# Two of four weight sums, and two of four activation sums, put on GpSimd in the feed-forward units

## The chip, the cores and the metric

The kernel runs on one core of a Trainium2 chip. A core has TensorE (PE: matrix products, results go to PSUM), VectorE (DVE) and ScalarE (ACT) for elementwise work, GpSimd (POOL), and SyncE (SP), which here only starts transfers. Each engine works through its own list of instructions in order and waits on semaphores for the others. The metric is the device time of one execution in microseconds (us). The kernel before takes 2019.6 us (median of three runs, 2017.96 to 2023.13).

## The reference

The reference is a decoder trunk of two layers over 512 tokens of width 1024 in float32. Each layer is: half a SwiGLU feed-forward, a mixer, half a SwiGLU feed-forward. The mixer of layer 0 is an SSD head group beside an mLSTM head group, that of layer 1 a sparse attention with a top-k selection. The change touches the four feed-forwards alone:

```
def swiglu(h, w_gate, w_up, w_down):
    return (jax.nn.silu(h @ w_gate) * (h @ w_up)) @ w_down

x = x + 0.5 * swiglu(rms_norm(x, ffn_norm[l, i]), w_gate[l, i], w_up[l, i], w_down[l, i])
```

The inner width is 2816, so `w_gate` and `w_up` are 1024 x 2816 and `w_down` is 2816 x 1024.

## The kernel before, in words

**Numbers in two parts.** Every operand of a product is split into a high part (rounded to the format that PE takes) and a low part (the rest), and `mm3` (lines 280 to 282) makes three matmuls of one product: high x high, high x low, low x high. A block of weights lands in a `raw` buffer (a ring of 4, `NRAW`), and its two parts go to a `form` buffer (a ring of 5, `NFORM`). There are two ways to make a form. `parts` lets ACT write the high part (line 500) and DVE the low part as the difference (line 502). The other, marked `summed`, lets ACT write the negated high part into the low place (line 529), then a transfer from POOL's queue adds the raw block to it (line 530), and ACT writes the high part (line 531).

**Units.** A feed-forward has 11 units of 256 inner columns, in groups of 4, 4 and 3 (`GROUPS`). Units 0 and 1 multiply plainly (`unit`). Units 2 to 10 (`unit_seven`), and the down projection of each group in two halves (`down`), use a 2 x 2 scheme with seven products in place of eight (`seven`). This makes 9 + 6 = 15 sevens in a feed-forward and 60 in the kernel. A seven takes four raw blocks b11, b21, b12, b22 and multiplies, in turn, forms of b11 (with A11), of b12 - b11 (S1), of b22 - b11' (S2), of b21 (A12), of b22 - b12 (S3), of b22 (S4), and of b21 - t2 (A22); b11' is the first difference and t2 the second. In the first half of a down projection the A12 product comes second. The four differences of raw blocks are `less` (line 648), which writes the first into b11, the second into a box t2, the third into b12, and the fourth into t2 again. Forms of b21 and b22 are made the `summed` way, the other five by `parts`.

**Streams.** The activations that a seven of gate and up multiplies with are seven forms of the normed stream, `xf`, made once in a feed-forward by `xforms` (two calls): four sums of 128 x 512 blocks in the tiles `ft`, numbered 4 (S1), 5 (S2), 6 (S3) and 7 (S4), and splits of all seven. Those of a down projection come from the hidden block of each unit (`forms`: sums of 128 x 256 blocks in `ft`, parts in `hid`). The down projection of a group can't begin to use a unit's `hid` before the unit's own last products have been evacuated (c12 and c21 in `unit_seven`), multiplied, and split.

**What sets the order.** The feed-forwards (and the attention) are not issued as they are written. `Plan` collects steps with an engine, a price and the keys that they read and write; `order` runs a list schedule over them: at each turn the step that can start first on its engine is taken, and by the earliest due time among those; PE keeps the written order of each stream. `issue` then hands the steps to the engines in that order. The prices are `v` for DVE (0.15 us + 1.05 ns for each element of a row) and `p` for POOL (0.1 us + 2.5 ns). The plan knows no contention between engines. The helper `vtt` (line 492) adds a two-input operation to DVE, or to POOL if its last argument is true; all these operations have line 495 in the profile. POOL's queue holds the 136 adding transfers of line 530, the adds of the squares for the norm (line 495, tile `ssq`), and work of the mixers. The kernel's ring of raw blocks has just the four of one seven, so each block of the next seven is loaded when its predecessor in the ring was last read.

Of the kernel before, what the change touches and what calls it, by code (L numbers as in the profile page):

```python
# [17 lines left out]
T = 512  # L18
# [195 lines left out]
class Trunk:  # L214
# [274 lines left out]
    def t(self, us, issue, reads, writes):  # L489
        self.plan.add("tensor", us, issue, reads, writes)  # L490
# [81 lines left out]
    def xforms(self, q0, tiles):  # L572


        (t, tk), (u, uk) = self.place(), self.place()
        which, xT, rrow, nc = self.which, self.xT, self.rrow, self.nc
        block = [lambda i=i: t()[:, 2 * i : 2 * i + 2] for i in range(4)] + [lambda i=i: u()[:, 2 * i : 2 * i + 2] for i in range(4)]
        bk = [[tk(2 * i), tk(2 * i + 1)] for i in range(4)] + [[uk(2 * i), uk(2 * i + 1)] for i in range(4)]
        for q in range(2):
            for m in range(2):  # L580
                k = 2 * (q0 + q) + m
                self.v(T, lambda q=q, m=m, k=k: nc.vector.scalar_tensor_tensor(
                    t()[:, 4 * m + q : 4 * m + q + 3 : 2], xT[:, k].rearrange("p (a b) -> p a b", a=2), self.gain(which, k),
                    rrow.rearrange("p (a b) -> p a b", a=2), op0=ALU.mult, op1=ALU.mult,
                ), self.xk(k) + ["rrow"], [tk(4 * m + q), tk(4 * m + q + 2)])
        key = lambda i, part, q: ("xf", self.count["xf"], i, part, q)

        def split(form, i):
            self.parts(
                T, lambda: tiles[form]()[:, 0, q0 : q0 + 2], lambda: tiles[form]()[:, 1, q0 : q0 + 2], block[i],  # L590
                [key(form, 0, q0), key(form, 0, q0 + 1)], [key(form, 1, q0), key(form, 1, q0 + 1)], bk[i],
            )

        tt = lambda o, x, y, op: self.vtt(T, block[o], block[x], block[y], op, bk[o], bk[x] + bk[y])
        split(self.A11, 0)
        tt(4, 1, 3, ALU.add)
        split(self.S1, 4)
        tt(5, 4, 0, ALU.subtract)
        split(self.S2, 5)
        split(self.A12, 2)  # L600
        tt(6, 0, 1, ALU.subtract)
        split(self.S3, 6)
        tt(7, 2, 5, ALU.subtract)
        split(self.S4, 7)
        split(self.A22, 3)
        return [
            (lambda i, q=q: (tiles[i]()[:, 0, q], tiles[i]()[:, 1, q]), lambda i, q=q: [key(i, 0, q), key(i, 1, q)])
            for q in (q0, q0 + 1)
        ]
# [11 lines left out]
    def seven(self, raws, xf, late, kept, evac):  # L621

        nc = self.nc
        b11, b21, b12, b22 = raws
        c11, c12, c21, c22 = evac
        nq = len(xf)
        i, two = "sum", self.box
        t2 = i, two[:, 0 : nq * 256].rearrange("p (n w) -> p n w", w=256)  # L630

        def mul(ps, block, form, start, summed=False, f=None, ss=(0, 1)):
            j, f = made = f or self.made(block, summed)
            ps, psk = ps
            for s in ss:
                col = slice(s * P, (s + 1) * P)
                for q in range(nq):
                    self.times(
                        ps, psk, s, (j, lambda q=q, col=col: (f[:, 0, q, col], f[:, 1, q, col])),
                        lambda q=q: xf[q][0](form), xf[q][1](form), start and q == 0, q == nq - 1, not start, H, 0.355,  # L640
                    )
            return made

        def keep(to, ps):
            (to, tok), (ps, psk) = to, ps
            self.s(T, lambda: nc.scalar.activation(to(), ps()[:, :, 0:H], AF.Copy), [(*psk, 0), (*psk, 1)], tok)

        def less(o, x, y):
            n = nq * 256
            self.vtt(n, lambda: o[1], lambda: x[1], lambda: y[1], ALU.subtract, [("raw", o[0])],  # L650
                     [("raw", x[0]), ("raw", y[0])])
            return o

        A, D = self.pair("pA", "pA"), self.pair("pD", "pB")
        mul(A, b11, self.A11, True)
        keep(kept[0], A)
        if late:
            B = self.pair("pB", "pB")
            mul(B, b21, self.A12, True, True)
            c11(B, kept[0])  # L660
            mul(D, less(b11, b12, b11), self.S1, True)
            keep(kept[2], D)
            mul(A, less(t2, b22, b11), self.S2, False)
            keep(kept[1], A)
            f22 = mul(D, b22, self.S4, False, True, ss=(0,))
            mul(A, less(b12, b22, b12), self.S3, False)
            c22(A, kept[2])
            mul(D, b22, self.S4, False, f=f22, ss=(1,))
            c12(D, kept[1])
        else:  # L670
            mul(D, less(b11, b12, b11), self.S1, True)
            keep(kept[2], D)
            mul(A, less(t2, b22, b11), self.S2, False)
            keep(kept[1], A)
            B = self.pair("pB", "pB")
            mul(B, b21, self.A12, True, True)
            c11(B, kept[0])
            mul(A, less(b12, b22, b12), self.S3, False)
            c22(A, kept[2])
            mul(D, b22, self.S4, False, True)  # L680
            c12(D, kept[1])
        mul(A, less(t2, b21, t2), self.A22, False)
        c21(A, None)

    def unit_seven(self, raws, xf):
# [1208 lines left out]
```

## Time and profile before

| what | us |
|---|---|
| median of three runs | 2019.6 |
| profiled execution, its own time | 2019.29 |
| its span, first to last instruction | 2017.6 |
| PE busy | 1984.4 (98%) |
| DVE busy | 1581.4 (78%) |
| ACT busy | 1170.2 (58%) |
| POOL busy | 270.1 (13%) |

The granted TensorE clock is 0.992 of full speed over the span. Busy time is the union of an engine's instructions; the ends of matmuls are modelled, so a busy PE can still have had small gaps. In the timeline a row gives the start, the length (of all instructions merged in it), engine, line, operation, what it writes and reads, and in brackets the idle time before it with what ended it. The feed-forwards lie at 0 to 345 us, 762 to 1092 us, 1093 to 1434 us and 1677 us to the end.

### The profile page before, as it was taken

What the parts mean: (1) busy time and instruction counts of PE and PEld (TensorE: products, weight loads), DVE (VectorE), ACT (ScalarE), POOL (GpSimd) and SP (SyncE); (2) the same over time, 40 slices, a digit from 0 to 9 for tenths busy, and PEclk for the clock granted to TensorE, in tenths of its full rate; (3) what the DMA queues carried; (4) which work ended last, traced back from release to release, by engine and by line L of the source; (5) the groups of instructions that cost most, each with busy time, mean ns of one, the idle gap of its engine ahead of it and who ended that gap; (6) DMA issues with size and microseconds to landing.
All of it is one profiled execution on the core that took longest, in us unless ns stands there. A gap on an engine that the chain in (4) does not pass through costs nothing.

```text
span 2017.6 us, 34412 instructions
## 1 busy us (share of the span) xinstructions
PE 1984.4 (98%) x13892; PEld 1800.6 (89%) x13892; DVE 1581.4 (78%) x2340; ACT 1170.2 (58%) x1716; POOL 270.1 (13%) x335
## 2 busy tenths in 40 slices
PE   8999999999999999999999999999999999999998
PEld 6999999787788888999998899999965678999998
DVE  6898878886547648988888898978679847988886
ACT  6666657442345434666565575756667644757565
POOL 1000101321101011010002010101215321101010
PEclk9999999999999999999999999999899999999999
DMA  7556566433331232666565356656754202656564
GB/s 210 136 148 167 150 164 148 125 107 115 103 96 63 82 97 63 168 157 162 155 152 149 94 148 167 161 153 160 191 116 105 53 16 69 157 158 165 150 168 115
DMA packets 214439, 265.49 MB, mean 132 GB/s; under 512 B 14140, under 2 KB 187400, under 8 KB 214280
## 3 DMA queue, kind: packets, MB, share of 16 engines
q1 hardware_dynamic: 193632, 190.87, 30.5%
q0 software_dynamic: 20448, 72.36, 19.2%
q8 instruction: 109, 1.79, 0.4%
q14 instruction: 50, 0.41, 0.1%
q10 hardware_dynamic: 200, 0.06, 0.0%
HBM read 188.77 MB, written 2.14 MB: 95 GB/s over the span
## 4 chain that ended last, share of the span: by engine, by line
PE 86%; DVE 5%; DMA 4%; issue 2%; ACT 1%; POOL 1%; SPq 0%; ACTq 0%; POOLq 0%; DVEq 0%
PE pA L281 9%; PE pA L280 9%; PE pA L282 9%; PE pD L280 5%; PE pD L281 5%; PE pD L282 5%; PE pB L280 2%; PE pB L281 2%; PE pB L282 2%; DMA form<-raw 2%; PE po L280 2%; PE po L282 2%; PE po L281 2%; PE ptok L280 2%; PE pu L282 2%
## 5 line engine op out<-in xcount | busy, mean ns | idle before, releaser
L502 DVE TENSOR_TENSOR form<-raw,form 128x1024 fp32r<-128x1024 f32 (+1 forms) x327 | 388.0, 1191 | 113.2 <-ACT form L500 112.3
L500 ACT ACTIVATE form<-raw 128x1024 fp32r<-128x1024 f32 (+1 forms) x327 | 334.6, 1027 | 177.3 <-DVE raw L495 120.6
L280 PE MATMUL pA<-xf,form 128*128 128x256 f32 x1152 | 322.1, 280 | 0.0
L281 PE MATMUL pA<-xf,form 128*128 128x256 f32 x1152 | 321.8, 279 | 0.0
L282 PE MATMUL pA<-xf,form 128*128 128x256 f32 x1152 | 321.4, 279 | 0.0
L495 DVE TENSOR_TENSOR raw<-raw 128x1024 f32<-128x1024 f32 (+2 forms) x241 | 283.6, 1180 | 17.4 <-DMA raw<-in_ffn_w_down 8.6
L530 POOL DMA_DIRECT2D form<-raw x136 | 116.9, 860 | 1202.7 <-ACT form L529 1142.4
L529 ACT ACTIVATE form<-raw 128x1024 fp32r<-128x1024 f32 (+1 forms) x136 | 140.1, 1031 | 140.3 <-PE pD L282 77.4
L280 PEld LDWEIGHTS pA<-xf,form 128*128 128x128 f32 x1152 | 216.4, 188 | 0.2
L282 PEld LDWEIGHTS pA<-xf,form 128*128 128x128 f32 x1152 | 216.1, 188 | 0.0
L281 PEld LDWEIGHTS pA<-xf,form 128*128 128x128 f32 x1152 | 215.8, 187 | 0.2
L281 PE MATMUL pA<-hid,form 128*128 128x256 f32 x704 | 198.6, 282 | 2.8 <-DVE hid L502 2.8
L280 PE MATMUL pA<-hid,form 128*128 128x256 f32 x704 | 198.8, 282 | 0.5 <-ACT hid L500 0.4
L282 PE MATMUL pA<-hid,form 128*128 128x256 f32 x704 | 197.4, 280 | 0.0
L280 PE MATMUL pD<-xf,form 128*128 128x256 f32 x576 | 161.2, 280 | 0.0
L281 PE MATMUL pD<-xf,form 128*128 128x256 f32 x576 | 161.2, 280 | 0.0
L282 PE MATMUL pD<-xf,form 128*128 128x256 f32 x576 | 161.0, 280 | 0.0
L495 DVE TENSOR_TENSOR ft<-ft 128x256 f32<-128x256 f32 (+2 forms) x288 | 146.1, 539 | 4.6 <-ACT ft L748 1.2
L531 ACT ACTIVATE form<-raw 128x1024 fp32r<-128x1024 f32 (+1 forms) x136 | 138.6, 1021 | 0.0
L281 PEld LDWEIGHTS pA<-hid,form 128*128 128x128 f32 x704 | 132.3, 188 | 4.7 <-DVE hid L502 4.6
L280 PEld LDWEIGHTS pA<-hid,form 128*128 128x128 f32 x704 | 132.6, 188 | 1.3 <-ACT hid L500 0.6
L282 PEld LDWEIGHTS pA<-hid,form 128*128 128x128 f32 x704 | 132.3, 188 | 0.0
(447 smaller groups left out, 5191.5 us busy)
## 6 DMA issues: line engine op xcount, KB each, us to landing
form<-raw POOLq DMA_DIRECT2D x120, 512.0 KB, 5.6
raw<-in_ffn_w_gate SPq DMA_DIRECT2D x88, 512.0 KB, 3.8
raw<-in_ffn_w_up SPq DMA_DIRECT2D x88, 512.0 KB, 4.0
raw<-in_ffn_w_down SPq DMA_DIRECT2D x64, 512.0 KB, 4.4
raw<-in_hy_w_in SPq DMA_DIRECT2D x44, 512.0 KB, 3.5
raw<-in_ffn_w_down SPq DMA_DIRECT2D x32, 384.0 KB, 3.4
raw<-in_hy_w_out SPq DMA_DIRECT2D x16, 512.0 KB, 3.3
form<-raw POOLq DMA_DIRECT2D x16, 384.0 KB, 4.2
```

The costliest lines, as they stand in the source:

```text
L280: mm(out, l[0], r[0], start=start, stop=False)
L281: mm(out, l[0], r[1], start=False, stop=False)
L282: mm(out, l[1], r[0], start=False, stop=stop)
L495: (self.p if pool else self.v)(n, lambda: e.tensor_tensor(out(), x(), y(), op=op), reads, writes)
L500: self.s(n, lambda: nc.scalar.activation(hi(), src(), AF.Copy), srck, hik)
L502: n, lambda: nc.vector.tensor_tensor(lo(), src(), hi().bitcast(F32), op=ALU.subtract), srck + hik, lok
L529: self.s(n, lambda: nc.scalar.activation(f()[:, 1], raw, AF.Copy, scale=-1.0), rawk, lok)
L530: self.plan.add("gpsimd", 0.85, lambda: nc.gpsimd.dma_start(f()[:, 1], raw, accum_op=ALU.add), rawk + lok, lok, 5.5)
L531: self.s(n, lambda: nc.scalar.activation(f()[:, 0], raw, AF.Copy), rawk, hik)
```

## The change

The third and the fourth of the four differences of raw blocks in every seven (b22 - b12, and b21 - t2), and the sums numbered 6 and 7 in `xforms` (for S3 and S4), are given to POOL. The plan prices them with `p` and orders all steps anew. What is computed is the same.

```
-        tt = lambda o, x, y, op: self.vtt(T, block[o], block[x], block[y], op, bk[o], bk[x] + bk[y])
+        tt = lambda o, x, y, op: self.vtt(T, block[o], block[x], block[y], op, bk[o], bk[x] + bk[y], o in (6, 7))
...
-        def less(o, x, y):
+        def less(o, x, y, pool=False):
             n = nq * 256
             self.vtt(n, lambda: o[1], lambda: x[1], lambda: y[1], ALU.subtract, [("raw", o[0])],
-                     [("raw", x[0]), ("raw", y[0])])
+                     [("raw", x[0]), ("raw", y[0])], pool)
             return o
...
-            mul(A, less(b12, b22, b12), self.S3, False)
+            mul(A, less(b12, b22, b12, True), self.S3, False)
...
-            mul(A, less(b12, b22, b12), self.S3, False)
+            mul(A, less(b12, b22, b12, True), self.S3, False)
...
-        mul(A, less(t2, b21, t2), self.A22, False)
+        mul(A, less(t2, b21, t2, True), self.A22, False)
```

In the changed program's lists POOL has 120 more operations on raw blocks (104 of 128 x 1024, 16 of 128 x 768, the last group of a feed-forward having three units) and 16 more on `ft` (128 x 512); DVE has as many fewer. On POOL they stand between the adding transfers, mostly one after each; where a group begins two stand together. The order of DVE, ACT and of SP's loads changes throughout the feed-forwards; that of PE only at the seam from the first feed-forward to the mixer of layer 0 and in the attention.

## The prediction

> **What bounds the kernel now.** I read the page's busy shares first, then the stages of the feed-forwards by windows, then the chain that ended last, and the timelines of one seven and of one group end.
>
> ```profile
> PE 1984.4 (98%) x13892; PEld 1800.6 (89%) x13892; DVE 1581.4 (78%) x2340; ACT 1170.2 (58%) x1716; POOL 270.1 (13%) x335
> ```
> ```profile
> 105.00:147.00 42.00, 40.90 (x343) 40.50 (x342) 38.83 (x49) 25.03 (x31) 3.43 (x4) 1.00 0.54 143
> ...
> 1184.00:1224.00 40.00, 39.64 (x332) 39.44 (x331) 36.78 (x46) 23.34 (x30) 3.40 (x4) 1.00 0.56 147
> 1224.00:1303.00 79.00, 79.00 (x673) 79.00 (x672) 66.48 (x82) 51.99 (x69) 6.87 (x9) 1.00 0.66 168
> ...
> sum 1270.00, PE 1264.42 PEld 1236.21 DVE 1090.10 ACT 804.78 POOL 112.13; mean PE 46.83 PEld 45.79 DVE 40.37 ACT 29.81 POOL 4.15
> ```
>
> The columns are span, then busy time of PE, weight loads, DVE, ACT and POOL. The last row sums 27 stretches that cover nearly all of the four feed-forwards: PE is idle for 5.6 of 1270 us there. From 1224 to 1303 us, four sevens, it is idle for nothing while DVE is busy for 84%. So relief of DVE can't buy much in these stages: at most those 5.6 us. Where PE does idle is where a group's down projection begins (the first two rows). The chain that ended last passes through DVE just there:
>
> ```profile
> 1400.39 0.70 DVE ft L495
> 1401.15 0.57 issue
> 1401.72 0.95 DVE form L502
> 1402.67 0.87 DVE raw L495
> 1403.54 0.61 DVE hid L502
> 1404.20 0.39 PE pA L281
> ```
>
> PE waits for the last unit's `hid`, and DVE makes it after a form and a raw difference. This is what the change touches: DVE is not the bound on average, but its latency is at twelve group ends (three in each feed-forward).
>
> **The change, part by part.** First, the work moved.
>
> ```profile
> L495 DVE TENSOR_TENSOR raw<-raw 128x1024 f32<-128x1024 f32 x208 | 253.2, 1220 | 16.4 <-DMA raw<-in_ffn_w_down 7.7 <-DMA raw<-in_ffn_w_up 6.7
> ...
> L495 DVE TENSOR_TENSOR ft<-ft 128x512 f32<-128x512 f32 x104 | 68.5, 686 | 0.9
> ...
> L495 DVE TENSOR_TENSOR raw<-raw 128x768 f32<-128x768 f32 x32 | 30.3, 953 | 1.0 <-DMA raw<-in_ffn_w_down 0.9
> ```
>
> DVE loses 104 x 1.220 + 16 x 0.953 + 16 x 0.686 = 126.9 + 15.2 + 11.0 = 153 us. On POOL no operation of 1024 elements is in the trace; the nearest are the adds of squares:
>
> ```profile
> L495 POOL TENSOR_TENSOR ssq<-ssq x23: 729/1597/2156, 350.1 to 1672.1; 128x512 f32<-128x512 f32 x17, 128x256 f32<-128x256 f32 x6
> ```
> ```profile
> L404 POOL TENSOR_TENSOR ssq<-ssq,sq x7: 1295/1345/1855, 709.0 to 759.5; 128x512 f32<-128x512 f32 x7
> ```
>
> The quickest take 0.729 us for 256 elements (the first row's minimum) and 1.295 us for 512, which is 2.21 ns for each further element; so I estimate 2.43 us for 1024 and 1.86 us for 768. POOL gains 104 x 2.43 + 16 x 1.86 + 16 x 1.295 = 303 us. It has the room (270 of 2017.6 us busy), so this by itself costs nothing.
>
> Second, what an operation of POOL does to DVE. Where the sums of squares run beside a busy DVE:
>
> ```profile
> 350.08 5.11 POOL L495 TENSOR_TENSOR ssq<-ssq 128x512 f32<-128x512 f32 x3 [5.10 <-ACT ssq L809]
> ```
> ```profile
> 349.87 0.74 DVE L798 SCALAR_TENSOR_TENSOR xgn<-raw,xgn 128x512 fp32r<-128x512 f32 x1
> 350.53 1.79 DVE L858 SCALAR_TENSOR_TENSOR raw<-ft,raw 128x512 f32<-128x512 f32 x1
> 352.24 0.68 DVE L495 TENSOR_TENSOR ft<-pA,ft 128x512 f32<-128x512 f32 x1
> 352.84 2.90 DVE L798 SCALAR_TENSOR_TENSOR xgn<-raw,xgn 128x512 fp32r<-128x512 f32 x2
> 355.66 0.68 DVE L858 SCALAR_TENSOR_TENSOR raw<-ft,raw 128x512 f32<-128x512 f32 x1
> ```
>
> The same DVE operation takes 1.79 us beside POOL and 0.68 us after it; two of line 798 take 2.90 us in place of 2 x 0.74. The one that reads PSUM and SBUF (`ft<-pA,ft`) stays at 0.68 us. So DVE operations with both inputs in SBUF wait for POOL's. DVE lost 1.11 + 1.42 = 2.53 us to three POOL operations that alone take 3 x 1.295 = 3.89 us: 0.65 us for each us of POOL. For 303 us that is 197 us lost against 153 us saved: DVE is not relieved but delayed by some 44 us, and its share of the 1270 us goes from 86% to about 89%. It still has room on average, and PE stays the bound in the middle of a group. The Trainium skill, SBUF — State Buffer, section Who interferes with whom, has the rule: a DVE instruction with two SBUF inputs contends with a GpSimd instruction that reads SBUF, and the later one blocks until the first is through. The trace agrees (1.79 against 0.68 us, and 0.68 us with one PSUM input).
>
> Third, the middle of a group, one seven of gate and up.
>
> ```profile
> 1246.99 0.28 PE L280 MATMUL pD<-xf,form 128*128 128x256 f32 x1
> ...
> 1269.60 0.28 PE L280 MATMUL pA<-xf,form 128*128 128x256 f32 x1
> ```
> ```profile
> 1260.38 1.23 DVE L495 TENSOR_TENSOR raw<-raw 128x1024 f32<-128x1024 f32 x1
> ...
> 1262.13 1.21 DVE L495 TENSOR_TENSOR raw<-raw 128x1024 f32<-128x1024 f32 x1
> 1263.36 1.23 DVE L502 TENSOR_TENSOR form<-raw,form 128x1024 fp32r<-128x1024 f32 x1
> 1264.62 1.23 DVE L495 TENSOR_TENSOR raw<-raw 128x1024 f32<-128x1024 f32 x1
> ```
> ```profile
> 1262.78 0.86 POOL L530 DMA_DIRECT2D form<-raw  x1 [12.79 <-ACT form L529]
> ```
>
> The four DVE rows are b22 - b11', b22 - b12 (moved), the low part of the S2 form, and b21 - t2 (moved). The S2 form is ready at 1264.6 us and PE starts on it at 1269.60 us: 5.0 us of slack, the least that I found on the weights' side. With the moved difference on POOL as soon as b22 has landed, b22 - b11' can wait for it (up to 2.43 us); the low part after it isn't blocked again, since b21 - t2 overwrites t2 and must wait for that low part. So at most half the slack goes. The adding transfer of b21, queued on POOL at 1262.78 us, now stands behind the moved difference (ready some 2.43 us after 1260.4, or up to 1.2 us later if DVE goes first): 0 to 1.3 us late. The release of b12 and b21, and with it SP's next loads, is late by about as much as POOL takes longer (1.2 us), once in each seven and not adding up. I cost the 60 sevens at nothing; if that cover is gone, each us by which a seven overruns costs up to 60 us.
>
> The 16 sums of `xforms` stand near the start of a feed-forward, ahead of the first seven's S3 and S4 products, and are covered by two plain units of PE work: nothing; uncovered, 16 x 0.65 x 1.295 = 13 us.
>
> Fourth, the group ends.
>
> ```profile
> 1300.18 1.22 DVE L495 TENSOR_TENSOR raw<-raw 128x1024 f32<-128x1024 f32 x1
> 1301.32 0.69 DVE L495 TENSOR_TENSOR ft<-pD,ft 128x512 f32<-128x512 f32 x1
> 1302.04 0.69 DVE L495 TENSOR_TENSOR ft<-ft 128x512 f32<-128x512 f32 x1
> 1302.65 1.22 DVE L495 TENSOR_TENSOR raw<-raw 128x1024 f32<-128x1024 f32 x1
> 1303.79 0.68 DVE L502 TENSOR_TENSOR hid<-ft,hid 128x512 fp32r<-128x512 f32 x1
> ```
> ```profile
> 1302.77 0.63 ACT L500 ACTIVATE hid<-ft 128x512 fp32r<-128x512 f32 x1 [0.18 <-DVE ft L495]
> ```
> ```profile
> 1303.52 0.29 PE L280 MATMUL pA<-hid,form 128*128 128x256 f32 x1
> ...
> 1304.60 0.28 PE L280 MATMUL pA<-hid,form 128*128 128x256 f32 x1
> ```
>
> The group's down projection starts at 1303.52 us with the units already there, and needs the last unit's `hid` with its tenth matmul, at 1304.60 us; `hid` is ready at 1303.79 + 0.68 = 1304.47 us. There is no slack, so what delays `ft<-ft` or `hid` (both with two SBUF inputs) is paid by PE in full. In the changed kernel b22 - b12 of the down projection's first seven runs on POOL beside these, from about 1300.2 us on. The price is a share of 2.43 us: at the measured 0.65, 1.58 us. Against it, the difference at 1302.65 us is no longer ahead of `hid`: ACT was done at 1303.40 us, so that frees 1303.79 - 1303.40 = 0.39 us. In the last groups, three units wide, 0.65 x 1.86 = 1.21 us stands against the whole 0.87 us of the chain shown above. The sum is 8 x (1.58 - 0.39) + 4 x (1.21 - 0.87) = 9.5 + 1.4 = 10.9 us. Bounds: nothing lost and all freed, -(8 x 0.39 + 4 x 0.87) = -6.6 us; the whole hold each time, 8 x 2.04 + 4 x 0.99 = +20.3 us. I take the measured share, since those rows are the same kind of operation on a DVE as dense.
>
> The reordered work at the seam to the mixer of layer 0 I cost at 0, between -3 and +3 us (half of the 5.6 us, either way). Sum: 2019.3 (the profiled execution, 0.3 below the median) + 10.9 = 2030.2 us.
>
> **The rivals.** (a) The whole hold: POOL takes the read first at each group end and keeps it through. This gives +20.3 us, 2039.6 us. For it speaks the 1.11 us that one DVE operation lost to one of 1.295 us (0.86 of it); against it that the next ones lost less. The rule cited above, taken as a block from start to end, gives this same time. (b) The sevens overrun: if the late t2, the late transfer and the late release eat more than the 5.0 us, PE waits in each seven, and the time is 60 us higher for each us beyond: 2040 us and more. Against it: I count some 2.4 + 1.3 us. (c) The other side: the moved difference is done before it matters. If b22 lands 2.43 us before DVE's `ft<-ft` at 1302.04 us, that is, if POOL starts by 1299.6 us, its hold lies under `ft<-pA` and `ft<-pD`, which read PSUM. Then only the freed time counts, -6.6 us, and the kernel takes 2012.7 us; with half of the ends so, 2019.3 + (10.9 - 6.6)/2 = 2021.5 us, no change. For it speaks that DVE made b22 - b11' at 1300.18 us with no wait, so b22 was there earlier. (d) That nothing is moved is excluded by the changed program's lists.
>
> **How the numbers follow.** No change means within 0.3%, about 6 us, of 2019.6 us, which is what a measurement of this kernel can tell. The forecast (2023 to 2036 us) gets 0.42; (a) and (b) together 0.22; (c) by halves 0.24, in full 0.12. Of the forecast 0.02 falls under the bound. So slower 0.42 + 0.22 - 0.02 = 0.62, same 0.24 + 0.02 = 0.26, faster 0.12. The range takes in (c) in full at 2012.7 us and (b) with an overrun of a tenth of a us beyond (a), 2039.6 + 6 = 2045.6 us. The forecast's own range is 2023 to 2036 us.
>
> **What would show it.** Right: POOL's differences at 2.4 us or more; DVE's `form<-raw,form`, `ft<-ft` and `hid` with means clearly above those of before, those from PSUM unchanged; PE idle longer just after the first `pA<-hid` of a group, by about 1 us, with DVE `hid` as releaser, and still none between 1224 and 1303 us. Wrong: DVE's busy time down by the whole 153 us (no contention), PE gaps at group ends gone, or gaps in each seven with a form as releaser. The forecast fails if the port's share differs much with the density of DVE's work, or if the new order puts `hid` elsewhere.

## The result, and the profile after

The changed kernel takes 2105.8 us (median of six runs, 2095.8 to 2106.5) against 2019.3 us before (six runs, 2017.96 to 2023.13). The ratio is 1.041, with a 95% interval of 1.039 to 1.043: by the medians 86 us slower. (The ratio is not the quotient of the medians; here the two differ by some 3 us.) The forecast was 2030.2 us, with a range that ended at 2045.6 us. The sign was right, the size too small by a factor of eight.

The profiled execution took 2105.76 us by its own time, with a span of 2104.0 us. First the busy shares of the page, then the shares of the chain that ended last.

```profile
PE 2010.4 (96%) x13892; PEld 1814.4 (86%) x13892; DVE 1659.3 (79%) x2204; ACT 1173.5 (56%) x1716; POOL 638.6 (30%) x471
...
PE 45%; DVE 23%; DMA 14%; ACT 7%; issue 6%; POOL 5%; SPq 0%; POOLq 0%; ACTq 0%; DVEq 0%
```

The same chain line of the kernel before:

```profile
PE 86%; DVE 5%; DMA 4%; issue 2%; ACT 1%; POOL 1%; SPq 0%; ACTq 0%; POOLq 0%; DVEq 0%
```

DVE has 136 instructions fewer and is busy for 78 us *longer*. The chain went from 86% PE to 45%; the rest runs through DVE, DMA and ACT. So PE no longer sets the time alone. (The share is a hint and no measure: in the run below with the streams' sums alone it is 71% PE, at an unchanged time.) Where the DVE time went is in the groups by shape (mean ns of one is the number after the busy time), first of the kernel after:

```profile
L502 DVE TENSOR_TENSOR form<-raw,form 128x1024 fp32r<-128x1024 f32 x287 | 414.7, 1452 | 127.8 <-ACT form L500 126.3
L495 DVE TENSOR_TENSOR raw<-raw 128x1024 f32<-128x1024 f32 x104 | 158.3, 1522 | 26.1 <-DMA raw<-in_ffn_w_up 22.9 <-DMA raw<-in_ffn_w_down 1.8
L495 DVE TENSOR_TENSOR ft<-ft 128x512 f32<-128x512 f32 x88 | 127.2, 1448 | 3.2 <-DVE ft L495 0.5
...
L495 DVE TENSOR_TENSOR ft<-pA,ft 128x512 f32<-128x512 f32 x60 | 41.1, 685 | 15.7 <-PE pA L282 15.7
...
L495 POOL TENSOR_TENSOR raw<-raw 128x1024 f32<-128x1024 f32 x104 | 308.2, 2964 | 616.4 <-DMA raw<-in_ffn_w_up 282.6 <-DVE form L502 148.8 <-DMA raw<-in_ffn_w_down 72.3
...
L495 POOL TENSOR_TENSOR raw<-raw 128x768 f32<-128x768 f32 x16 | 34.7, 2168 | 32.6 <-DVE form L502 30.3 <-DMA raw<-in_ffn_w_down 2.3
L495 POOL TENSOR_TENSOR ft<-ft 128x512 f32<-128x512 f32 x16 | 29.1, 1820 | 45.1 <-DVE ft L495 16.9 <-PE pg L282 14.6 <-DVE ft L582 10.1
```

and two of the kernel before that the prediction did not show:

```profile
L502 DVE TENSOR_TENSOR form<-raw,form 128x1024 fp32r<-128x1024 f32 x287 | 349.9, 1225 | 107.7 <-ACT form L500 107.2
...
L495 DVE TENSOR_TENSOR ft<-pA,ft 128x512 f32<-128x512 f32 x60 | 41.4, 691 | 35.9 <-PE pA L282 35.3
```

The three largest groups of DVE operations with both inputs in SBUF got longer: 1225 to 1452 ns, 1220 to 1522 ns, 686 to 1448 ns. The one with an input in PSUM did not (691 and 685 ns). Not every operation with two SBUF inputs is hit: `hid<-ft,hid` of 128 x 512 goes from 685 to 767 ns only, that of 128 x 256 from 418 to 417. The means hide two kinds: of the 104 differences of 128 x 1024 left on DVE, 87 took some 1.22 us as before, and 17 took longer, most of them by 2.2 us. Of all DVE operations of lines 495 and 502, 114 took longer than the shortest of their kind before (by over 0.08 us), 111 of them by more than 1 us and none by more than 2.3. So the loss is made of rare, long holds. The moved operations take 308.2 + 34.7 + 29.1 = 372 us on POOL. DVE, less the 153 us taken from it, would be busy for 1581.4 - 153 = 1428 us and is busy for 1659 us, so it lost 231 us: 0.62 us for each us of POOL.

Now the stages. The columns are as in the prediction's table of windows; the last three numbers of a row are the granted clock, the DMA share and GB/s.

```profile
106.00:153.00 47.00, 42.73 (x336) 42.30 (x335) 38.07 (x39) 24.22 (x30) 13.93 (x8) 0.93 0.51 125
112.00:119.00 7.00, 6.90 (x35) 6.90 (x36) 6.36 (x9) 4.35 (x7) 3.08 (x2) 0.55 0.53 122
1228.00:1271.00 43.00, 40.28 (x338) 39.78 (x337) 37.88 (x38) 23.79 (x29) 13.84 (x8) 1.00 0.54 137
1271.00:1352.00 81.00, 80.48 (x679) 79.87 (x678) 70.37 (x72) 51.46 (x67) 31.82 (x18) 1.00 0.67 163
```

The two down projections, 42 and 40 us wide before, are 47 and 43 us wide, with PE idle for 4.3 and 2.7 us (before: 1.1 and 0.4). Four sevens of gate and up took 79 us and take 81. And the second row shows a thing that the prediction left out: for 7 us after a stall, PE ran at a granted clock of 0.55.

A busy PE hides small gaps, so I also took the distances from one matmul's start to the next in the feed-forwards. The table is for the matmuls of the sevens (256 columns); at full rate their distance is 0.118 us. Distances over 0.3 us I call gaps, those from 0.15 to 0.3 us half-rate matmuls, and I add up what is beyond 0.118 us. The name half-rate is wide: of the 23.8 us after, 13.9 lie in eight stretches of 14 to 27 such matmuls in a row, which is the clock; the others stand alone or in short rows and can be small waits.

| us in the feed-forwards | before | after |
|---|---|---|
| gaps in the first product of a group's down projection | 5.0 (10 gaps) | 35.9 (26) |
| gaps elsewhere | 0.3 | 40.2 (51) |
| half-rate matmuls | 2.3 | 23.8 |
| sum | 7.6 | 99.9 |

The difference is 92 us, against 86 us between the two profiled executions; the 6 us between them I did not attribute. (An expectation below says 33 us for the group starts: it counts only the gaps that begin in the first 4 us.)

**A group's end.** DVE, POOL and PE in the timeline, at the first group of the kernel after:

```profile
102.23 0.69 DVE L495 TENSOR_TENSOR ft<-pA,ft 128x512 f32<-128x512 f32 x1
104.42 1.23 DVE L502 TENSOR_TENSOR form<-raw,form 128x1024 fp32r<-128x1024 f32 x1 [1.51 <-ACT form L500]
105.57 3.41 DVE L495 TENSOR_TENSOR raw<-raw 128x1024 f32<-128x1024 f32 x1
108.90 0.68 DVE L495 TENSOR_TENSOR ft<-pD,ft 128x512 f32<-128x512 f32 x1
109.62 0.69 DVE L495 TENSOR_TENSOR ft<-ft 128x512 f32<-128x512 f32 x1
110.22 1.22 DVE L502 TENSOR_TENSOR form<-raw,form 128x1024 fp32r<-128x1024 f32 x1
111.36 0.68 DVE L502 TENSOR_TENSOR hid<-ft,hid 128x512 fp32r<-128x512 f32 x1
```
```profile
104.66 3.24 POOL L495 TENSOR_TENSOR raw<-raw 128x1024 f32<-128x1024 f32 x1 [1.42 <-DMA raw<-in_ffn_w_down]
```
```profile
107.17 0.28 PE L282 MATMUL pA<-hid,form 128*128 128x256 f32 x1
111.02 0.38 PE L280 MATMUL pA<-hid,form 128*128 128x256 f32 x1 [3.58 <-ACT hid L500]
112.10 0.58 PE L281 MATMUL pA<-hid,form 128*128 128x256 f32 x1 [0.69 <-DVE hid L502]
```

POOL's b22 - b12 begins at 104.66 us. DVE's b22 - b11' begins at 105.57 us, and ends 1.08 us after POOL's end (107.90 us): it was held for 2.2 us. `ft<-pD` stands behind it, though it reads PSUM and is itself not slowed, then `ft<-ft` and `hid`. The place in the list counts too. In this group of the kernel before, b22 - b11' (106.23 us) came behind `ft<-pD` and `ft<-ft`:

```profile
104.91 0.68 DVE L495 TENSOR_TENSOR ft<-pD,ft 128x512 f32<-128x512 f32 x1
...
106.23 1.22 DVE L495 TENSOR_TENSOR raw<-raw 128x1024 f32<-128x1024 f32 x1
```

Now all 3.41 us of it stand ahead of them. In the kernel after, PE has multiplied nine times with `hid`, and stops from 107.17 us (its last start) to 111.02 us, and again for the low part. The other groups are alike: in 11 of the 12, one raw difference or low part of a form, held for 1.4 to 2.2 us, stands on DVE in the 5 us before the down projection's first matmul or reaches into it; in the twelfth `hid` itself is held.

**The middle of a seven.** In gate and up, PE also stops where the product S3 begins. DVE, POOL, ACT and PE in the last feed-forward:

```profile
1937.16 2.89 DVE L502 TENSOR_TENSOR hid<-ft,hid 128x512 fp32r<-128x512 f32 x1
1939.98 2.27 DVE L495 TENSOR_TENSOR ft<-ft 128x512 f32<-128x512 f32 x5
```
```profile
1936.19 3.31 POOL L495 TENSOR_TENSOR raw<-raw 128x1024 f32<-128x1024 f32 x1 [0.97 <-DVE form L502]
```
```profile
1941.67 0.63 ACT L500 ACTIVATE hid<-ft 128x512 fp32r<-128x512 f32 x1 [2.77 <-DVE ft L495]
1942.21 0.58 ACT L646 ACTIVATE ft<-pD 128x512 f32<-128x512 f32 x1
...
1944.46 0.58 ACT L646 ACTIVATE ft<-pA 128x512 f32<-128x512 f32 x1
```
```profile
1945.10 0.38 PE L280 MATMUL pA<-xf,form 128*128 128x256 f32 x1 [1.11 <-ACT ft L646]
```

A `hid` of DVE, a part of an earlier unit's forms, is held by POOL (2.89 us in place of 0.68). Its next sums in `ft` are late, and ACT waits for them for 2.77 us with a `hid` at the head of its list. Behind that stand the evacuations of line 646. The one of pA starts at 1944.46 us; S3, which accumulates on pA, needs it, and PE waits 1.11 us. S2, the product evacuated there, had ended on PE by 1941.2 us, so the evacuation could have come some 3.3 us earlier. Neither the weights nor DVE's forms are late here. The waits, as the profile adds them up, for PE and then ACT:

```profile
PE pA L280 <- ACT hid L500: 20.2, 11, 3.6
PE pA L280 <- ACT ft L646: 17.9, 24, 1.5
PE pA L281 <- DVE hid L502: 10.0, 12, 3.3
PE pD L282 <- DMA form<-raw: 5.0, 7, 1.3
```
```profile
ACT hid L500 <- DVE ft L495: 101.1, 65, 4.8
```

and the row of ACT before:

```profile
ACT hid L500 <- DVE ft L495: 22.8, 28, 1.8
```

The first and third rows of PE are group ends, the second is this evacuation. The fourth is a weight form that comes late: in six of the seven waits its adding transfer had stood right behind a difference in POOL's queue. The kernel before has no such wait in its sevens.

### The profile page after: what moved, and what is told of

Its sections match the earlier page's. It is cut to its first block, busy times and chain, and to the rows that moved or that the text cites. A ratio compares the mean times of both kernels' runs of the same rounds, so it can differ in the third digit from the quotient of the medians.

```text
span 2104.0 us, 34425 instructions
## 1 busy us (share of the span) xinstructions
PE 2010.4 (96%) x13892; PEld 1814.4 (86%) x13892; DVE 1659.3 (79%) x2204; ACT 1173.5 (56%) x1716; POOL 638.6 (30%) x471
## 4 chain that ended last, share of the span: by engine, by line
PE 45%; DVE 23%; DMA 14%; ACT 7%; issue 6%; POOL 5%; SPq 0%; POOLq 0%; ACTq 0%; DVEq 0%
DVE form L502 8%; DMA form<-raw 6%; DVE ft L495 5%; POOL raw L495 4%; DVE raw L495 4%; DMA raw<-in_ffn_w_down 4%; DMA raw<-in_ffn_w_up 4%; PE pA L281 3%; PE pA L280 3%; PE pA L282 3%; ACT form L500 3%; PE po L280 2%; PE po L282 2%; PE po L281 2%; DVE xf L502 2%
## 5 line engine op out<-in xcount | busy, mean ns | idle before, releaser
L502 DVE TENSOR_TENSOR form<-raw,form 128x1024 fp32r<-128x1024 f32 (+1 forms) x327 | 456.6, 1404 | 138.5 <-ACT form L500 136.9
L495 POOL TENSOR_TENSOR raw<-raw 128x1024 f32<-128x1024 f32 (+1 forms) x120 | 342.9, 2858 | 648.9 <-DMA raw<-in_ffn_w_up 282.6
L500 ACT ACTIVATE form<-raw 128x1024 fp32r<-128x1024 f32 (+1 forms) x327 | 335.4, 1029 | 244.3 <-DVE raw L495 176.1
L280 PE MATMUL pA<-hid,form 128*128 128x256 f32 x704 | 203.9, 290 | 24.1 <-ACT hid L500 20.2
L281 PE MATMUL pA<-hid,form 128*128 128x256 f32 x704 | 203.1, 288 | 10.0 <-DVE hid L502 10.0
L495 DVE TENSOR_TENSOR ft<-ft 128x256 f32<-128x256 f32 (+2 forms) x272 | 206.4, 785 | 7.8 <-ACT ft L748 1.3
L495 DVE TENSOR_TENSOR raw<-raw 128x1024 f32<-128x1024 f32 (+2 forms) x121 | 181.9, 1504 | 28.6 <-DMA raw<-in_ffn_w_up 22.9
L282 PE MATMUL pA<-hid,form 128*128 128x256 f32 x704 | 201.5, 286 | 0.0
L529 ACT ACTIVATE form<-raw 128x1024 fp32r<-128x1024 f32 (+1 forms) x136 | 139.9, 1031 | 110.3 <-PE pD L282 61.2
L280 PEld LDWEIGHTS pA<-hid,form 128*128 128x128 f32 x704 | 136.0, 193 | 28.5 <-ACT hid L500 22.4
L500 ACT ACTIVATE hid<-ft 128x512 fp32r<-128x512 f32 (+1 forms) x176 | 96.8, 571 | 101.2 <-DVE ft L495 101.1
L281 PEld LDWEIGHTS pA<-hid,form 128*128 128x128 f32 x704 | 136.4, 194 | 12.5 <-DVE hid L502 12.5
```

Source lines behind the costliest of these rows:

```text
L280: mm(out, l[0], r[0], start=start, stop=False)
L281: mm(out, l[0], r[1], start=False, stop=False)
L282: mm(out, l[1], r[0], start=False, stop=stop)
L495: (self.p if pool else self.v)(n, lambda: e.tensor_tensor(out(), x(), y(), op=op), reads, writes)
L500: self.s(n, lambda: nc.scalar.activation(hi(), src(), AF.Copy), srck, hik)
L502: n, lambda: nc.vector.tensor_tensor(lo(), src(), hi().bitcast(F32), op=ALU.subtract), srck + hik, lok
```

## The experiments

Four theories stood. *The port*: POOL's reads hold up DVE's operations with two inputs in SBUF, and that alone makes the loss. *The way*: the moved sums are late since POOL takes longer, or the new order of all lists is worse. *The clock*: the stalls are short, but PE runs at half rate after them. *Addition*: the parts of the change each cost their share. Unless said otherwise, ratios are to the kernel before on the same chip (its medians there are 2017.5 to 2020.7 us).

### POOL as busy, but without reading

```
+        if pool == "fill":
+            def fill():
+                e, cut = self.nc.gpsimd, lambda t: t[:, 0:1, 0:4]
+                e.tensor_tensor(cut(out()), cut(x()), cut(y()), op=op)
+                for _ in range(3):
+                    e.memset(out(), 0.0)
+            self.p(n, fill, reads, writes)
```

> The changed kernel, in its order, with each operation that was moved to GpSimd replaced by work of about the same length that hardly reads SBUF: a difference of 4 elements of a row on the same blocks (so the waits stay) and three fills of the whole block with zeros (the third and fourth difference of each seven, and the sums for S3 and S4, are left out of the result). Theory P (VectorE's operations with two SBUF inputs wait for GpSimd's reads): VectorE's form<-raw,form comes back to about 1.22 us and the time to 2015 to 2040 us. Rival O (the new order and the longer way over GpSimd, 2.4 to 3 us in place of 1.2, are what costs): 2095 to 2110 us, with form<-raw,form means that do not matter.

Measured: 2019.8 us, ratio 0.9998 (0.9982 to 1.0015). The groups (line 511 here is line 502), and the busy shares:

```profile
L499 POOL MEMSET raw<- 128x1024 f32 x312 | 298.3, 956 | 18.1
...
L511 DVE TENSOR_TENSOR form<-raw,form 128x1024 fp32r<-128x1024 f32 x287 | 350.1, 1222 | 215.8 <-ACT form L509 215.5
```
```profile
PE 1979.7 (98%) x13892; PEld 1798.5 (89%) x13892; DVE 1444.9 (72%) x2204; ACT 1169.1 (58%) x1716; POOL 702.5 (35%) x879
```

A moved sum here takes 3 x 0.956 us of fills and the small difference, longer than the 2.96 us of the real one; the order of all lists is that of the kernel after; the writes are as many, and more. Yet `form<-raw,form` is at 1222 ns, and no time is lost. In this run no difference, sum or part of the large groups takes longer than before. So the loss is neither the longer way nor the order alone: it needs POOL's reads of SBUF. And the relief of DVE, from 1581 to 1445 us, shortened the kernel by nothing.

### The order of after, with all work on DVE

```
-        e = self.nc.gpsimd if pool else self.nc.vector
+        e = self.nc.gpsimd if pool is True else self.nc.vector   # the moved sums: "planned"
```

> The changed kernel's order of all steps, planned with GpSimd's prices, but the moved differences and sums are executed by VectorE at the places which the plan gives them. Theory P: no GpSimd reads beside VectorE, so 2018 to 2040 us, VectorE's means as before. Rival O (the order that the plan makes is bad by itself, because ScalarE's and VectorE's lists put other things ahead of the hidden block's parts and of the evacuations): above 2060 us.

Measured: 2032.9 us, ratio 1.0052 (1.0031 to 1.0072). Gaps at group starts are 14.6 us, half-rate matmuls 7.6 us. So the new order with the work back on DVE costs 12 us (2032.9 - 2020.7), and with the work away from DVE and no reads, in the run above, nothing. The order by itself is no large part of the 86 us, but at the group starts it does count: 14.6 us of gaps against 5.0.

### The kernel before, with idle differences on POOL

```
+            def adding():
                 nc.gpsimd.dma_start(f()[:, 1], raw, accum_op=ALU.add)
+                if idle is not None:                      # in a seven
+                    for _ in range(n // 128):
+                        nc.gpsimd.tensor_tensor(idle, idle, idle, op=ALU.subtract)
```

> The kernel before, in its order and with all differences on VectorE; after each adding transfer of a seven (120 of them) GpSimd also does eight subtractions of 128 x 128 on a tile of its own that nobody else touches (1024 elements of a row in all, as many as one moved difference, some 3 us). Theory P: VectorE loses about as much as in the changed kernel and has not been spared the 153 us, so the time goes to 2050 to 2150 us. Rival O: nothing in the order or in any dependence has changed, so 2017 to 2026 us.

Measured: 2054.4 us, ratio 1.0166 (1.0134 to 1.0199), with nothing moved and nobody waiting for the subtractions. Eight of them took 6.8 us, not the 3 us expected, and the adding transfers stand behind them in POOL's queue; but PE waited for those for only 1.2 us in the sevens.

```profile
L536 POOL TENSOR_TENSOR idle<-idle 128x128 f32<-128x128 f32 x928 | 786.8, 848 | 63.3
```
```profile
L502 DVE TENSOR_TENSOR form<-raw,form 128x1024 fp32r<-128x1024 f32 x287 | 381.4, 1334 | 61.5 <-ACT form L500 61.0
```

Reading alone costs time, then. DVE is busy for 1693.8 us by this run's page, 112 us more than before, for 787 us of short operations on POOL: 0.14 us per us, far from 0.62, and half the 231 us that the theory had. And it is busy for longer than in the kernel after (1659.3 us), while the loss is 34 us and not 86. So DVE's busy time is not what sets the time. The holds differ: here 663 DVE operations of lines 495 and 502 take longer, counted in the same way, 639 of them by 0.08 to 0.25 us; in the kernel after it was 114, nearly all by more than 1 us. In these two runs many small delays did less harm than fewer long ones. No run varied the length of POOL's operations by itself.

### The weights alone, and the streams alone

```
+        tt = lambda o, x, y, op: self.vtt(..., bk[x] + bk[y])            # weights alone
```
```
+            mul(A, less(b12, b22, b12), self.S3, False)                  # streams alone: no True
```

> The changed kernel with the sums of the normed stream's forms (xforms) back on VectorE; the 120 differences of weight blocks stay on GpSimd. If the weights' differences carry the loss: 2090 to 2108 us. If the dense start of each feed-forward, where the 16 sums of xforms stand, carries a good part of it: 2040 to 2085 us.

> The kernel before with only the 16 sums of xforms (128 x 512) on GpSimd. At 0.65 us lost for each of 16 x 1.8 us of GpSimd, VectorE loses some 19 us and is spared 11, spread over plain units in which TensorE has work: 2017 to 2026 us. If each of these waits reaches TensorE: 2030 to 2040 us.

Measured: the weights alone 2097.1 us, ratio 1.0385 (1.0355 to 1.0415); the 16 sums of the streams alone 2019.7 us, ratio 1.0002 (0.9985 to 1.0019). The loss is the 120 weight sums'. The streams' 16 cost nothing by themselves; on top of the weights' sums they may cost some (2105.8 - 2097.1 = 8.7 us by the medians, but the intervals of the two ratios overlap).

### The third difference alone, and the fourth alone

```
+        mul(A, less(t2, b21, t2), self.A22, False)                       # third alone
```
```
+            mul(A, less(b12, b22, b12), self.S3, False)                  # fourth alone (both places)
```

> Only the third difference of each seven (b22 - b12, 60 operations) on GpSimd. Theory: this one starts with the landing of b22, together with VectorE's b22 - b11, and so delays the evacuation behind it and the hidden block at the group ends; the long waits of TensorE at the start of a down projection and the half clock after them stay, the waits between the B and the A product in the middle of the sevens mostly go: 2045 to 2070 us. Rival (any read of GpSimd costs alike, wherever it stands): half of the 86 us, 2062 us, with both kinds of waits halved.

> Only the fourth difference of each seven (b21 - t2, 60 operations) on GpSimd. Theory: this one runs beside VectorE's sums for the hidden block; ScalarE waits for those with the hidden block's high part at the head of its list, the evacuation of the A product (line 646) stands behind, and TensorE waits for it between the B and the A product; those waits stay (some 20 us), the long waits at the group starts mostly go: 2035 to 2060 us. Rival (any read costs alike): 2062 us with both kinds halved.

Measured: the third alone 2057.8 us, ratio 1.0180 (1.0143 to 1.0218); the fourth alone 2049.8 us, ratio 1.0149 (1.0117 to 1.0180). The waits of PE, third alone and then fourth alone:

```profile
PE pA L280 <- ACT hid L500: 18.0, 9, 4.0
PE pA L281 <- DVE hid L502: 9.5, 12, 1.4
```
```profile
PE pA L281 <- DVE hid L502: 7.4, 9, 1.8
...
PE pA L280 <- ACT hid L500: 4.2, 5, 1.8
```

The third makes most of the group ends (gaps there 33.2 us, against 14.7 us with the fourth alone), as the timeline above has it. But PE hardly waits for the evacuation of line 646 in either (2.0 us in 2 waits, 1.4 us in 3): in gate and up PE's stop ahead of S3 is missing with the third alone and 0.4 us with the fourth alone, against 19.2 us with both. And 37.9 + 29.9 = 68 us is less than the 77 us of both. I had the fourth alone as the maker of this wait; that fell. DVE's delay does reach ACT with the fourth alone:

```profile
ACT hid L500 <- DVE ft L495: 71.0, 61, 2.5
```

(37.4 us with the third alone, 22.8 before, 101.1 with both.) What one hold in a seven does not do is bring the evacuation so late that PE stops ahead of S3. What makes the second hold decide was not tried by itself.

### Matmuls in the stall, to hold the clock

```
+                    if warm and s == ss[0] and q == nq - 1:    # first product of each down, warm=21
+                        for _ in range(warm):
+                            nc.tensor.matmul(ps()[:, 1, H:T], l, r, start=True, stop=True, skip_group_check=True)
```

(shortened: the loop is a step of the plan, ahead of the last unit's first matmul.)

> The changed kernel, with 21 matmuls that go nowhere (into the unused columns of the same PSUM tile, 21 x 0.118 = 2.5 us at full clock) put on TensorE just ahead of the first matmul of each down projection that needs the last unit's hidden block, where TensorE idles. Theory C (the half clock after these stalls, which I reckon at some 20 us in all, comes from TensorE's idling): the stretches at half clock after the group starts go and the time falls by 10 to 20 us, to 2085 to 2095 us. Rival: the clock falls for another reason, or the stalls were shorter than the matmuls: 2100 to 2130 us.

Measured: 2098.1 us, ratio 1.0390 (1.0354 to 1.0425). The cores' rows, of the kernel after and of this one:

```profile
core 0: 2104.0 us, clock 0.986
```
```profile
core 0: 2102.7 us, clock 0.992
```

The granted clock is that of before again, although 29.7 us of matmuls are added; half-rate matmuls fall from 23.8 to 14.0 us, and of the eight stretches three are left (13.9 to 4.6 us). By the medians the time falls by 2105.8 - 2098.1 = 7.7 us, 3 us short of the expected range; but the two ratios, 1.039 and 1.041, have intervals that overlap, so the fall in time is not clear of noise. What the profiles do show is that the long stretches at half clock cost some 14 us of the sevens, and that the matmuls took most of it away. The time at the group starts stays: 5.4 us of gaps and the 29.7 us of added matmuls are as long as the 35.9 us of gaps were. So do the stops ahead of S3, where nothing was added (line 653 here is line 646):

```profile
PE pA L280 <- ACT ft L653: 19.3, 25, 1.8
```

### A plan that knows of the port

```
+        if pool == "port":                         # a slot of DVE in the plan, that issues nothing
+            port = [("port", self.ports)]
+            self.plan.add("vector", 1.5e-3 * n, lambda: None, reads, port)
+            reads, pool = reads + port, True
```

> The changed kernel with the same operations on GpSimd, but the plan also reserves VectorE for 1.5 ns an element (1.54 us for 1024) ahead of each, so that it no longer believes VectorE free beside them, and orders all engines' lists by that. Theory (a large part of the waits of TensorE in the middle of the sevens comes from lists ordered for a VectorE that is free: ScalarE waits for the hidden block's sums with an evacuation behind): the waits between the B and the A product, some 19 us, shrink to a few, the group starts stay: 2060 to 2090 us. Rival (the waits are there in whatever order): 2095 to 2115 us.

Measured: 2101.3 us, ratio 1.0417 (1.0400 to 1.0434); the expected 2060 to 2090 us was missed. Gaps at group starts fell from 35.9 to 6.3 us, the stop ahead of S3 from 19.2 to 7.3 us, but others came in their place, 20.0 us within products of pD with `hid` (lines 651 and 507 here are 646 and 502):

```profile
PE pA L280 <- ACT ft L651: 17.3, 20, 3.5
PE pD L281 <- DVE hid L507: 10.0, 10, 2.7
```

The slots are the plan's guess of the hold, before each moved sum. The holds are still there, and in this list, with one wait out of the way, another came. That speaks against one badly placed step as the cause, but one list does not prove it.

### The first half of each down projection left on DVE

```
-            mul(A, less(b12, b22, b12, True), self.S3, False)
+            mul(A, less(b12, b22, b12, not late), self.S3, False)     # likewise the fourth
```

> The changed kernel, with the two differences on VectorE in the first half of each down projection (12 of the 60 sevens: those whose weights are made while the last unit of the group is still being finished), on GpSimd in the other 48. Theory: TensorE's long waits at the group starts (33 us against 5 in the kernel before) go, and with them most of the 20 us lost at half clock; the waits in the middle of the sevens stay: 2050 to 2070 us. Rival (loss in proportion to the operations on GpSimd, 48 of 60): 2085 to 2092 us.

Measured: 2067.9 us, ratio 1.0255 (1.0238 to 1.0272), as expected. In its profile (of an execution of 2059.3 us, the shortest of the four) gaps at group starts are 13.5 us, half-rate matmuls 8.5 us; the stops in gate and up stay:

```profile
PE pA L280 <- ACT ft L646: 18.2, 21, 2.0
```

So the moved sums of 12 of the 60 sevens cost about 2105.8 - 2067.9 = 38 us of the 86 by the medians, and those of the other 48 sevens (with the streams) the 50 us that stay. No version beat the kernel before.

## Why the prediction was right and wrong

**Right: DVE is not relieved.** The size of the hold, 0.65 us of DVE for each us of POOL from one place in the trace of before, came out as 0.62 over the whole kernel (0.58, if the DVE time of the run without reads is taken as base: (1659.3 - 1444.9)/372). That the two are so near is in part luck, for they divide by different things: 0.65 by what POOL's operations take undisturbed, 0.62 by what they took. On like terms it is 0.65 against 231/303 = 0.76, or 2.53/5.11 = 0.50 against 0.62. The kinds of operations that wait, and the one that doesn't, were right, though the short ones were hardly hit. DVE's net gain in busy time was put at 44 us and measured as 78 us. POOL's operations themselves became longer: 2.96 us on average beside DVE, where I had taken 2.43 us for one that runs undisturbed (the shortest in the trace take 2.39). The Trainium skill, SBUF — State Buffer, section Who interferes with whom, also says that a GpSimd instruction which only writes does not contend with such a DVE instruction; the run with the fills agrees (1222 ns against 1225).

**Wrong: the 60 sevens at nothing.** This is the step that failed. I looked for slack where the weights' forms reach PE (5.0 us), and most of the forms do still come in time: PE waits for a late adding transfer for 5.0 us in all, in 7 waits. So this part of rival (b) did come, but small. I did not follow the *other* work of the same DVE: the sums and parts of the previous units' `hid`, which are queued on DVE and ACT between those of the weights. In the middle of a seven their delay does not reach PE by their own result; it reaches it by the order of ACT's list, where a late `hid` stands ahead of an evacuation. Gaps away from group starts are 40 us, of which 19 us by this one wait; the other 21 us are spread over many places and were not followed one by one. The alternative that I had named, rival (b), was a late weight form too: it left room for a loss of this size (60 us for each us of overrun in every seven) and had, but for those 5.0 us, the wrong place. "It still has room on average" was the wrong question: DVE at 87% from 1271 to 1352 us has room on average, and still each hold of 2 us stands in an in-order list that others wait on.

**Mis-sized: the group ends.** The mechanism was right: POOL's b22 - b12 holds DVE just there, and `hid` is late. The term was +10.9 us for twelve ends, 0.9 us each; measured are 30.9 us more of gaps, 2.6 us for each end. Two parts of it were wrong. The hold is a whole one and not the average share of 1.58 us: it was 2.2 us at 105.57 us, above even the 2.04 us net of rival (a). And nothing was freed: in all eight groups of four units an operation of 1.22 us, mostly the low part of a form, still stands between `ft<-ft` and `hid`, since the plan made a new order. The order also put b22 - b11' ahead of `ft<-pD` in the first group: `ft<-pD` came 2.67 us after the down projection's first matmul, where in the same group before it had come 0.48 us ahead of it (104.91 and 105.39 us). I priced one average hold in the order of before. Nor did the freed time of DVE count for anything elsewhere: the run that has it and no reads gained nothing.

**Left out: the clock.** After seven of the stalls at group starts PE ran on at about half clock, 0.21 us for each matmul, and an eighth stretch followed a stop of 3.25 us at 2076.40 us, where PE transposes the finished stream (`pot`, line 886). These eight cost 13.9 us, and matmuls in the stalls took 9.3 us of it away. The Trainium skill, TensorE: Matmul & The Clock Gate, Part 1, has half rate follow an idle window of about 3.4 us; the stop of 3.85 us at 107.17 us agrees, but stretches of half clock also followed stops of 2.4 us (at 235.1 and 868.8 us, from the start times, each with a second one of 1.1 us behind it), shorter than that. With the third difference alone, a stretch followed stops of 1.34 and 0.88 us (at 862.94 us), and after those of 2.31 and 1.08 us in the group at 1228.56 us PE ran on at full rate. So the length of a stop alone does not tell. The same part has a second failure mode, where many small idle times between groups of matmuls bring half rate; the page gives no length for it, and no run here tells the two apart.

**Right: the streams' sums at nothing** (1.0002), and rival (c) fell as a whole: without POOL's reads and with all relief left, the time was that of before. There was no gain in this change to be had.

**What stays open.** Why two holds in a seven cost more than the sum of each alone was not separated. That ACT's list makes the stop ahead of S3 is read from the timeline and the waits; taking the evacuation out from behind `hid` was not tried. Nor was the same work on POOL cut into shorter operations.

## What to carry to other kernels

Work taken off a busy engine is worth nothing while another one is the bound, and here it was worse than nothing: POOL's reads held up DVE, so the time of the two did not add up. Price a move by the time that it takes from the engine that it is meant to relieve, and by the length of one hold rather than by the average share. When an engine's time is stretched in many small places, do not look for slack along one chain only: follow everything that stands in the same in-order list, and what stands behind it in the lists of the engines that wait for it. A run in which the second engine is as busy but reads nothing, and one with the same order and no move, separate contention from order in two runs.

## What the runs showed of the hardware that was not expected

- POOL is slowed as well: an operation of 128 x 1024 with two inputs took 2.96 us on average beside DVE and 2.39 us at best, one of 128 x 768 2.17 and 1.83 us.
- POOL's fills of the same buffers, 0.956 us each and 312 of them, cost DVE nothing (1222 ns for `form<-raw,form`, 1225 before).
- The loss differs much with the length of POOL's operations: 0.62 us of DVE per us in the kernel after, where most are of 1024 elements, 0.14 for rows of short ones of 128 elements (848 ns each). A DVE operation that was held lost 1 to 2.3 us beside the long ones and mostly 0.1 to 0.2 us beside the short ones.
- Stops of PE of 2.4 to 3.9 us, most with a shorter one behind them, were in eight cases followed by 3.4 to 6.8 us at half clock. With 21 matmuls put into each of the stops at group starts, the mean granted clock was 0.992 and not 0.986.
